# Later adaLN steps wait for the first FFN's norm and are spread over its down projections; one chunk's columns come within the output projection

## The chip, the core and the metric

One Trainium2 (trn2) chip, one core. The metric is the device time of one execution in microseconds (us); before the change it is 1256.7 us, the median of 3 runs (1254.57 to 1257.02).

## What is computed

A backbone of two layers over 512 latent tokens of width 1024, with 256 context tokens that feed only layer 0's keys and values. Layer 0 mixes with windowed grouped-query attention, layer 1 with a short gated convolution. Cut to what matters here:

```python
def layer(i, h, c, ...):
    sh1, sc1, g1, sh2, sc2, g2 = split(silu(c) @ ada_w[i] + ada_b[i], 6)     # adaLN: 6 chunks of 1024
    h = h + g1 * mixer_i(rms_norm(h, norm_mix[i]) * (1 + sc1) + sh1)
    a = rms_norm(h, norm_ffn[i]) * (1 + sc2) + sh2
    g, u = split(dwconv3(a @ w_up[i], ffn_conv[i]), 2)                      # w_up 1024 x 5632
    return h + g2 * ((silu(g) * u) @ w_down[i])                             # w_down 2816 x 1024
```

The change touches the adaLN vectors: per layer `silu(c)`, 1024 long, times a 1024 x 6144 matrix, in six chunks of 1024 outputs (0 and 1: shift and scale of the mixer's norm, 2: its gate, 3 and 4: shift and scale of the FFN's norm, 5: its gate).

## The kernel before, in words

All data are feature-major: the state `h` is eight tiles of 128 features x 512 tokens. A product in float32 is made of three TensorE (PE) matmuls on values split in a high and a low part (`mm3`, L196 to L198). So each weight that arrives (`wraw`, 128x1024) is split by ScalarE (ACT, `whi`, L164) and VectorE (DVE, `wlo`, L165) before PE can use it. With `n` pieces of 1024 inputs, one `proj` of one output tile of 128 x 512 is 8 x 3 matmuls.

**The adaLN vectors.** A chunk is made in eight steps, one per 128 inputs. A step loads two tiles `araw` of 128x512 (SP's queue, L244 in the FFN, L672 in attention, four buffers). GpSimd (POOL) multiplies each by a column of `silu(c)` (L258) and adds it to one of two accumulators `adaacc` (L260); a chunk's first step multiplies straight into the accumulator. When a chunk is done, PE transposes each half (four 128x128, L265, into the PSUM bank `qt`), and VectorE reduces it to columns and adds the bias (L270, L271, in `ada_columns`). Chunks 0 and 1 of layer 0 are made elsewhere. Chunks 2 to 4 of layer 0 (24 steps) are made within attention, chunk 5 of layer 0 and all six of layer 1 (56 steps, 112 tiles) within the first FFN.

**Attention** is written out by hand: the string `ORDER` names each step in the order in which the instructions are issued (`with tc.manual_schedule()`). In it `ad` loads an adaLN step, `ap` is the multiply and addition of one half, `AT` and `AR` are a half's transposes and columns; `T`, `C`/`c`, `V` are the probabilities' transposes, copies and value products; `Ri` or `ri` (ACT or GpSimd) spreads a pair's reciprocal denominators, which PE transposes (`RT`); `N`, `Nh`, `Nl` normalise a pair of heads and split the result, `Nl` on GpSimd (L666).

Everything after attention is ordered by the Tile scheduler, which takes instructions as they become ready and follows the program's order within that.

**Output projection** (`out_proj`). The first four output tiles come from weights that are in place (`lead`, 4 x 24 matmuls, kt by kt across the four), the other four in halves of 256 tokens (the tail), so that the norm of the first half (`norm_half`) begins while PE does the second. `sumsq_add` (L207) sums the squares of `h`, on GpSimd for output tiles 1 and 2 and on VectorE for the others. `rstd` makes the reciprocal root with matmuls over the features (L215) and transposes (L225), in layer 0's FFN norm by ACT's root and VectorE's reciprocal (L222), in later norms by VectorE and a power on GpSimd (L218, L219). `modulate` (L233 to L235) writes the normed, modulated activation in its two parts: VectorE, ACT, VectorE.

**First FFN** (`ffn`). 44 up projections in 22 pairs (gate and value), in thirds of 8, 8 and 6 pairs; after each third its part of the down projection, eight output tiles. The first two pairs run as four pieces in halves of the tokens, so that the norm's second half can be made beside the first. After each pair but the first, `tail0` calls three `ada_step`, as long as there are any, and at the pairs in `COLS_AT` it turns a finished chunk into columns. SP issues weights and adaLN tiles from one queue in the order that the scheduler has fixed, and a load of a tile waits there for its buffer.

Layer 1 has the same output projection, norm and first projection, with no adaLN steps beside them.

Of the kernel before, what the change touches and what calls it, by code (L numbers as in the profile page):

```python
# [41 lines left out]
for _k, _w in (("c", 16), ("gmix", 16), ("adab", 2 * 6 * KT), ("gffn", 16), ("fconv", 2 * 3 * 2 * NF), ("sconv", 3 * KT),  # L42
# [19 lines left out]
    wh5 qa0.2 kD0.0.0 Q1.1.0 kl0.0 qa0.3 qs0.3 wl5 kD0.0.1 kT1.1 kh1.1 ap2.0 hT0 kD1.1.0 qd0.3 wr9 Q1.0.1 wr10 hh0 kl1.1 hl0 kD1.1.1 Q1.0.2
    qp0.3 wl7 S0.0 wr11 Q1.0.3 M0.0.1 ap1.1 M0.0.0 E0.0.1 Q1.1.1 qr1.0 qs1.0 ap2.1 ad3 S0.1 E0.0.0 qd1.0 Q1.1.2 M0.1.0 qa1.0 ad4 Q1.1.3 M0.1.1
    E0.1.0 qp1.0 hT1 qr1.1 qs1.1 S0.3 E0.1.1 Q1.2.0 M0.3.0 ap3.0 hh1 Q1.2.1 M0.3.1 E0.3.0 hl1 E0.3.1 S0.2 qa1.1 qd1.1 Q1.2.2 M0.2.1 qp1.1 Q1.2.3
    M0.2.0 E0.2.1 Dd0 E0.2.0 ap4.0 S1.0 qr1.2 T0.0.1 De0 qs1.2 hT2 C0.0.1 M1.0.1 T0.0.2 qa1.2 hh2 V0.0.1 M1.0.0 C0.0.2 T0.0.3 ap3.1 E1.0.1 Rd0
# [865 lines left out]
```

## Time and profile before

| what | us |
|---|---|
| median of 3 runs | 1256.7 (1254.57 to 1257.02) |
| the profiled execution | 1254.22 |
| its span, first to last instruction | 1252.1 |
| mean granted TensorE clock of the span | 0.989 |
| busy: PE / DVE / ACT / POOL | 1208.0 / 762.5 / 480.5 / 399.1 |

The page splits the span by engines, then into 40 slices, then follows the chain of work that ended last. What is busy on the average says little here: TensorE is busy nearly throughout, and what it misses lies in a few stages. The stages in the text are read off the timeline of TensorE: attention ends at 245.43 us, the half-width tail of the output projection begins at 273.12, the first FFN projection ends at 342.63, and the half-width tail of the first FFN's last third begins at 685.13. Layer 1's counterparts are 859.11 (tail) and 907.53 (end of the first projection).

### The profile page before, as it was taken

How to read it: one execution, taken by the hardware profiler on the slowest of the kernel's cores; microseconds unless marked ns; L12 is line 12 of the kernel's file. 1: busy time of each engine (PE TensorE's matmuls, PEld its weight loads, DVE VectorE, ACT ScalarE, POOL GpSimd, SP SyncE). 2: the span in 40 equal slices, each digit the busy share in tenths (PEclk: the TensorE clock that was granted, in tenths of full speed). 3: DMA queues.
4: the chain of work that ended last, by engine and by line, in shares of the span. 5: the costliest groups of instructions: out<-in, count | busy, mean ns of one | idle time of the engine just before them, and what ended most of it. 6: DMA issues, size and time to landing. Idle time of an engine off the chain costs nothing.

```text
span 1252.1 us, 16546 instructions
## 1 busy us (share of the span) xinstructions
PE 1208.0 (96%) x6414; PEld 983.6 (79%) x6414; DVE 762.5 (61%) x1126; ACT 480.5 (38%) x785; POOL 399.1 (32%) x360
## 2 busy tenths in 40 slices
PE   8999999987699999979999999999999999999998
PEld 6677666677688788858888988889988888888888
DVE  3678877549987547763586754443686445553552
ACT  4435777614253223321333442232454224422430
POOL 0039757759905609996092000001000000000000
PEclk8999999999899999989999999999999999999999
DMA  9445322355444534556253233222243333332211
GB/s 365 153 132 167 119 81 87 123 183 166 162 160 128 192 92 155 191 193 209 86 168 104 83 118 101 93 93 69 68 138 97 101 92 94 101 102 85 80 38 68
DMA packets 58382, 157.61 MB, mean 126 GB/s; under 512 B 6592, under 2 KB 8640, under 8 KB 58304
## 3 DMA queue, kind: packets, MB, share of 16 engines
q1 hardware_dynamic: 58304, 156.56, 38.3%
q8 instruction: 50, 0.82, 0.3%
q14 instruction: 28, 0.23, 0.1%
HBM read 152.86 MB, written 2.10 MB: 124 GB/s over the span
## 4 chain that ended last, share of the span: by engine, by line
PE 78%; DVE 8%; POOL 8%; issue 2%; DMA 2%; ACT 1%; SPq 0%; POOLq 0%; DVEq 0%; ACTq 0%
PE ps_s L197 10%; PE ps_s L198 10%; PE ps_s L196 10%; PE ps_pt L198 5%; PE ps_pt L197 5%; PE ps_pt L196 5%; POOL adaacc L260 4%; PE ps_oa L655 3%; PE ps_pt L636 3%; PE ps_s L575 3%; PE ps_oa L197 3%; PE ps_qt L197 3%; PE ps_qt L198 3%; PE ps_qt L196 3%; PE ps_oa L196 3%; PE ps_oa L198 2%
## 5 line engine op out<-in xcount | busy, mean ns | idle before, releaser
L165 DVE TENSOR_TENSOR wlo<-wraw,whi 128x1024 fp32r<-128x1024 f32 (+2 forms) x194 | 230.3, 1195 | 168.2 <-ACT whi L164 163.2
L164 ACT CAST whi<-wraw 128x1024 fp32r<-128x1024 f32 (+2 forms) x194 | 183.3, 953 | 340.3 <-PE ps_s L197 141.6
L260 POOL TENSOR_TENSOR adaacc<-adaacc,araw 128x512 f32<-128x512 f32 x140 | 199.4, 1429 | 9.0
L197 PE MATMUL ps_s<-a,whi 128*128 128x512 f32 (+1 forms) x512 | 190.4, 372 | 7.4 <-DVE a L235 7.4
L196 PE MATMUL ps_s<-a,whi 128*128 128x512 f32 (+1 forms) x512 | 190.2, 371 | 0.0
L198 PE MATMUL ps_s<-a,wlo 128*128 128x512 f32 (+1 forms) x512 | 190.1, 371 | 0.0
L258 POOL TENSOR_SCALAR araw<-araw,cs 128x512 f32<-128x512 f32 x140 | 128.8, 922 | 11.8 <-DMA araw<-in_ada 11.7
L197 PEld LDWEIGHTS ps_s<-a,whi 128*128 128x128 f32 x512 | 97.1, 190 | 24.4 <-DVE a L235 8.4
L198 PEld LDWEIGHTS ps_s<-a,wlo 128*128 128x128 f32 x512 | 97.3, 190 | 16.2
L196 PEld LDWEIGHTS ps_s<-a,whi 128*128 128x128 f32 x512 | 97.1, 190 | 16.2
L196 PE MATMUL ps_s<-g,whi 128*128 128x512 f32 (+1 forms) x264 | 91.9, 348 | 0.0
L198 PE MATMUL ps_s<-g,wlo 128*128 128x512 f32 (+1 forms) x264 | 91.7, 347 | 0.0
L197 PE MATMUL ps_s<-g,whi 128*128 128x512 f32 (+1 forms) x264 | 91.6, 347 | 0.0
L196 PE MATMUL ps_pt<-a,whi 128*128 128x512 f32 (+1 forms) x240 | 88.9, 370 | 0.0
L197 PE MATMUL ps_pt<-a,whi 128*128 128x512 f32 (+1 forms) x240 | 88.8, 370 | 0.0
L198 PE MATMUL ps_pt<-a,wlo 128*128 128x512 f32 (+1 forms) x240 | 88.6, 369 | 0.0
L164 ACT CAST g<-f 128x512 fp32r<-128x512 f32 x52 | 32.3, 620 | 124.0 <-DVE f L812 123.4
L744 DVE SCALAR_TENSOR_TENSOR h<-ps_s,ada,h 128x512 f32<-128x512 f32 (+1 forms) x40 | 25.6, 644 | 79.9 <-PE ps_s L198 79.7
L584 DVE CUSTOM_DVE_ANT_0 e<-ps_s,mask,nsink 128x512 f32<-128x512 f32 (+1 forms) x64 | 53.8, 873 | 14.8 <-PE ps_s L575 13.6
L811 ACT ACTIVATE f<-f 128x512 f32<-128x512 f32 x44 | 27.8, 633 | 89.8 <-DVE f L735 89.7
L207 POOL TENSOR_TENSOR f<-f,t 128x512 f32<-128x512 f32 x6 | 9.4, 1571 | 161.9 <-ACT t L206 161.9
L258 POOL TENSOR_SCALAR adaacc<-araw,cs 128x512 f32<-128x512 f32 x20 | 15.4, 774 | 140.6 <-PE ps_qt L265 127.0
(282 smaller groups left out, 2618.9 us busy)
## 6 DMA issues: line engine op xcount, KB each, us to landing
wraw<-in_wup SPq DMA_DIRECT2D x88, 512.0 KB, 3.6
araw<-in_ada SPq DMA_DIRECT2D x160, 256.0 KB, 2.7
wraw<-in_wdown SPq DMA_DIRECT2D x32, 512.0 KB, 3.6
wraw<-in_wsc SPq DMA_DIRECT2D x24, 512.0 KB, 3.5
gw<-in_ada SPq DMA_DIRECT2D x16, 512.0 KB, 9.0
wraw<-in_wqkv SPq DMA_DIRECT2D x12, 512.0 KB, 5.6
wraw<-in_wdown SPq DMA_DIRECT2D x16, 384.0 KB, 3.1
wraw<-in_wo SPq DMA_DIRECT2D x8, 512.0 KB, 3.8
```

Of the source, the lines that this page charges most:

```text
L164: act.copy(out=hi, in_=raw)
L165: vec.tensor_tensor(out=lo, in0=raw, in1=hi.bitcast(F32), op=ALU.subtract)
L196: pe.matmul(out=ps, lhsT=wh, rhs=ah, start=start, stop=False)
L197: pe.matmul(out=ps, lhsT=wh, rhs=al, start=False, stop=False)
L198: pe.matmul(out=ps, lhsT=wl, rhs=ah, start=False, stop=stop)
L258: pool.tensor_scalar(out=w if kt else a, in0=w, scalar1=c_, scalar2=1.0, op0=ALU.mult, op1=ALU.mult)
L260: pool.tensor_tensor(out=a, in0=a, in1=w, op=ALU.add)
L575: pe.matmul(out=s[t][:, i, :w], lhsT=q2s[p][x][HALF[t], cl], rhs=KEYS[p // 4][(p // 2 + t) % 2][y][HALF[t], ks_], start=(n == 0), stop=(n ...
L584: vec.tensor_tensor_reduce(out=e[:, :n].rearrange("p (a b) -> p a b", a=np_), in0=s[:, :np_, :w], in1=mb.rearrange("p (a b) -> p a b", a=n ...
L636: pe.transpose(out=pt[:, q:q + P], in_=es[p, b, t][0][:, o:o + P], identity=ident)
L655: pe.matmul(out=r["po"][HALF[t], b0:b0 + n], lhsT=V[:, j, p // 2, :], rhs=pf[:, t * n:(t + 1) * n], start=first, stop=not r["left"])
L811: act.activation(out=cv[0], in_=cv[0], func=AF.Silu)
```

## The change

- `ORDER` is written anew. The 24 adaLN steps stand in another place, the transposes and columns of its third chunk (`AT2`, `AR2`: chunk 4, the scale of the FFN's norm) are no longer in it, and `Ri`/`ri` are dealt out otherwise (before GpSimd for pairs 1 to 6, now for 1, 4, 6 and 7). That chunk's accumulators are tiles of the `g` ring.
- Those transposes and columns come in `out_proj` behind the residuals of its first four output tiles (`cols`).
- The first multiply of the first FFN's steps that is ordered so by hand waits for the last VectorE instruction of that FFN's norm (`add_manual_dep`).
- In the first FFN two steps follow each pair, and one step follows each output tile of the down projections of the first two thirds (`after`). A finished chunk becomes columns two calls later.

Of `ORDER` one line and its counterpart; the rest of the diff is whole but for blank context:

```diff
-    c7.1.1 ap21.0 V7.1.4 ad22 V7.1.3 V7.1.1 N7 ad23 Nh7 Nl7 ap22.1 ap23.1 ap22.0 AT2.1 AR2.1 ap23.0 AT2.0 AR2.0
+    ap22.0 V6.1.1 M7.3.0 V6.1.5 V6.1.4 M7.3.1 E7.3.0 T7.0.0 ap23.0 T7.0.2 N6 E7.3.1 S7.2 c7.0.0 Nh6 c7.0.2 V7.0.0 Nl6 T7.0.1 M7.2.1 V7.0.2
...
+    Rc7 T7.1.5 c7.1.1 V7.1.2 C7.1.5 T7.1.4 V7.1.1 C7.1.4 V7.1.5 V7.1.4 N7 Nh7 Nl7
@@ modulate
-        vec.scalar_tensor_tensor(out=lo, in0=n, scalar=sh, in1=hi.bitcast(F32), op0=ALU.add, op1=ALU.subtract)
+        return vec.scalar_tensor_tensor(out=lo, in0=n, scalar=sh, in1=hi.bitcast(F32), op0=ALU.add, op1=ALU.subtract)
@@ ada_step
-            ada_mult_add(acc[half], raws[half], kt)
+            ins = ada_mult_add(acc[half], raws[half], kt)
+            after = adastate.pop("after", None)
+            if after is not None:
+                tc.add_manual_dep(ins.ins, after.ins.name, DEP, reason="the norm has VectorE's port for itself")
@@ ada_mult_add
-        pool.tensor_scalar(out=w if kt else a, in0=w, scalar1=c_, scalar2=1.0, op0=ALU.mult, op1=ALU.mult)
+        ins = pool.tensor_scalar(out=w if kt else a, in0=w, scalar1=c_, scalar2=1.0, op0=ALU.mult, op1=ALU.mult)
...
+        return ins
@@ ap_
-                accs[ch, hf] = ap.tile([P, 512], F32, tag="aacc", name=nm("adaacc"), bufs=2)
+                accs[ch, hf] = ap.tile([P, 512], F32, tag="aacc", name=nm("adaacc"), bufs=2) if ch < 2 else g(F32)
@@ norm_half
-                modulate(h[kt][:, hf], r, smod[:, n["slot"], kt:kt + 1], ...
+                n["end"] = modulate(h[kt][:, hf], r, smod[:, n["slot"], kt:kt + 1], ...
@@ out_proj
                     residual(m, ps[m], gate)
                     done(m, FULL)
+                cols()
             tail = 4 if nxt is not None or last else 0
             for m in range(len(lead), KT - tail):
                 ps = proj([wpiece(src(m), n)], ah, al)[0]
                 residual(m, ps, gate)
                 done(m, FULL)
+                if after is not None:
+                    after(1)
@@
-        scale_cols(smod[:, 2, :], ada[0][:, 4, :], pc("gffn", 0, 8))
+        def last_cols():
+            for hf in range(2):
+                ada_columns(0, 4, hf, ada_transpose(accs[2, hf]))
+            scale_cols(smod[:, 2, :], ada[0][:, 4, :], pc("gffn", 0, 8))
@@ ffn
-                    if tail is not None:
-                        tail(j)
+                    if tail is not None and j:
+                        tail(2)
...
-                out_proj(lambda m: wdown_d[layer, m, :, j0 * P:j1 * P], (j1 - j0) * P, hh, hl, gate, nx, fin)
+                out_proj(lambda m: wdown_d[layer, m, :, j0 * P:j1 * P], (j1 - j0) * P, hh, hl, gate, nx, fin, after=None if fin else tail)
@@
-        def tail0(j):
-            for _ in range(3 if j else 0):
+        def tail0(n):
+            late.append(len(adadone))
+            if late[-3] and adadone:
+                ada_cols()
+                late[-2:] = [v - 1 for v in late[-2:]]
+            if "first" not in adastate:
+                adastate["first"] = adastate["after"] = nf["end"]
+            for _ in range(n):
                 if fsteps:
                     ada_step(*fsteps.pop(0))
-            if j in COLS_AT:
-                ada_cols()
```

How the instructions move, at three places. Tiles carry a number of their own in each program; `L265` became `L269`, `L258` `L261`, `L260` `L263`, `L666` `L670`; `L244` and `L172` are the same.

TensorE, the lead of the output projection (L265/L269 are the transposes of chunk 4, `g_1768` and `g_2883` the attention's output). Before, in the lead's second kt, between its third and fourth output tile (the other set stands behind the first output tile of the third kt):

```order
L196 MATMUL ps_s_2963<-g_1768,whiA_1546 128x512
L197 MATMUL ps_s_2963<-g_1769,whiA_1546 128x512
L198 MATMUL ps_s_2963<-g_1768,wloA_1547 128x512
L265 MATMUL ps_qt_2885<-ident,adaacc_2505 128x128 x4
L196 MATMUL ps_s_2964<-g_1768,whiA_1586 128x512
```

With the change, at the lead's end and the beginning of the half-width tail:

```order
L196 MATMUL ps_s_2949<-g_2883,whiA_1604 128x512
L197 MATMUL ps_s_2949<-g_2884,whiA_1604 128x512
L198 MATMUL ps_s_2949<-g_2883,wloA_1605 128x512
L269 MATMUL ps_qt_3060<-ident,g_2287 128x128 x4
L196 MATMUL ps_oa_3075<-g_1540,whi_2913 128x256
```

The transposes moved from within the lead to behind it; the second set moved likewise, into the first piece of the tail.

GpSimd, from the last subtraction of attention (L666/L670) on; `adaacc_2505` and `adaacc_2544` belong to chunk 4, `adaacc_3643` and `adaacc_3644` to the first chunk of the first FFN. Before:

```order
L666 TENSOR_TENSOR g_2876<-t_2869,g_2875 128x512
L258 TENSOR_SCALAR araw_2863<-araw_2863,cs 128x512
L260 TENSOR_TENSOR adaacc_2505<-adaacc_2505,araw_2863 128x512
L258 TENSOR_SCALAR araw_2873<-araw_2873,cs 128x512
L260 TENSOR_TENSOR adaacc_2505<-adaacc_2505,araw_2873 128x512
L258 TENSOR_SCALAR araw_2861<-araw_2861,cs 128x512
L260 TENSOR_TENSOR adaacc_2544<-adaacc_2544,araw_2861 128x512
L258 TENSOR_SCALAR araw_2871<-araw_2871,cs 128x512
L260 TENSOR_TENSOR adaacc_2544<-adaacc_2544,araw_2871 128x512
L258 TENSOR_SCALAR adaacc_3643<-araw_3639,cs 128x512
L258 TENSOR_SCALAR adaacc_3644<-araw_3641,cs 128x512
```

With the change, from the last addition of chunk 4 (`g_2287` is one of its accumulators) on:

```order
L263 TENSOR_TENSOR g_2287<-g_2287,araw_2651 128x512
L670 TENSOR_TENSOR g_2787<-t_2766,g_2786 128x512
L612 COPY t_2840<-den_2604 128x512
L670 TENSOR_TENSOR g_2884<-t_2881,g_2883 128x512
L261 TENSOR_SCALAR araw_3647<-araw_3647,cs 128x512
L261 TENSOR_SCALAR araw_3649<-araw_3649,cs 128x512
L207 TENSOR_TENSOR f_2929<-f_2929,t_3049 128x512
L207 TENSOR_TENSOR f_2929<-f_2929,t_3053 128x512
L261 TENSOR_SCALAR adaacc_3643<-araw_3639,cs 128x512
L261 TENSOR_SCALAR adaacc_3644<-araw_3641,cs 128x512
L263 TENSOR_TENSOR adaacc_3643<-adaacc_3643,araw_3647 128x512
```

Chunk 4's last four tiles now stand ahead of the last subtraction, and of the FFN's steps only two multiplies stand ahead of the two sums of squares (L207). The multiply into `adaacc_3643` is the one that waits for the norm.

SP, the loads of the first FFN from its first adaLN tiles on (`wraw<-in_wup` are up-projection weights, one per projection). Before:

```order
L244 DMA araw_3655<-in_ada 128x512
L244 DMA araw_3657<-in_ada 128x512
L172 DMA wraw_3364<-in_wup 128x1024
L244 DMA araw_3743<-in_ada 128x512
L244 DMA araw_3745<-in_ada 128x512
L172 DMA wraw_3663<-in_wup 128x1024
L244 DMA araw_3751<-in_ada 128x512
L172 DMA wraw_3696<-in_wup 128x1024
```

With the change (`wraw_3941` is the last of eight weights that follow each other, `wraw_3364` the first; fifteen adaLN tiles follow, of which the last three stand here):

```order
L172 DMA wraw_3880<-in_wup 128x1024
L172 DMA wraw_3941<-in_wup 128x1024
L244 DMA araw_3735<-in_ada 128x512
```

```order
L244 DMA araw_4017<-in_ada 128x512
L244 DMA araw_4019<-in_ada 128x512
L244 DMA araw_4025<-in_ada 128x512
L172 DMA wraw_3972<-in_wup 128x1024
L244 DMA araw_4027<-in_ada 128x512
L244 DMA araw_4109<-in_ada 128x512
L244 DMA araw_4111<-in_ada 128x512
L172 DMA wraw_4033<-in_wup 128x1024
L172 DMA wraw_4064<-in_wup 128x1024
```

The first eleven weights now stand ahead of all but four adaLN tiles; the twelfth (`wraw_3972`) stands behind 19 of them and the thirteenth (`wraw_4033`) behind 22.

## Rows read from the trace of the kernel before

**Rows 1.** The page: busy time of two engines (share of the span, instructions), and the engines' shares of the chain of work that ended last.

```profile
PE 1208.0 (96%) x6414; PEld 983.6 (79%) x6414; DVE 762.5 (61%) x1126; ACT 480.5 (38%) x785; POOL 399.1 (32%) x360
...
PE 78%; DVE 8%; POOL 8%; issue 2%; DMA 2%; ACT 1%; SPq 0%; POOLq 0%; DVEq 0%; ACTq 0%
```

**Rows 2.** The view by stages: start and end, length, busy us of PE, its weight loads, DVE, ACT and POOL with their instructions, granted clock (1.00 is full), DMA share, GB/s.

```profile
84.00:245.40 161.40, 159.99 (x1142) 108.33 (x1140) 126.86 (x265) 105.55 (x230) 121.22 (x120) 1.00 0.35 110
245.40:273.10 27.70, 23.12 (x103) 18.21 (x102) 8.28 (x12) 5.58 (x7) 13.13 (x14) 1.00 0.60 200
273.10:342.80 69.70, 52.89 (x398) 51.05 (x397) 62.07 (x66) 23.11 (x46) 66.92 (x57) 0.93 0.50 166
342.80:682.00 339.20, 330.50 (x1459) 268.69 (x1459) 215.47 (x246) 116.77 (x156) 185.25 (x152) 0.99 0.47 154
859.10:907.50 48.40, 47.46 (x397) 47.04 (x396) 27.87 (x62) 18.03 (x38) 1.86 (x2) 1.00 0.18 56
```

**Rows 3.** What TensorE waited for between 240 and 600 us: total, number of waits, longest.

```profile
PE ps_oa L196 <- ACT g L164: 8.0, 2, 7.1
PE ps_s L197 <- DVE a L235: 7.4, 5, 2.5
PE ps_qt L265 <- POOL adaacc L260: 4.6, 2, 2.6
PE ps_pt L215 <- DVE f L207: 3.7, 1, 3.7
PE ps_qt L225 <- DVE rcol L222: 2.6, 1, 2.6
```

**Rows 4.** The same between 840 and 925 us (layer 1's output projection, norm and first projection).

```profile
PE ps_pt L225 <- POOL rcol L219: 0.5, 1, 0.5
PE ps_s L225 <- POOL rcol L219: 0.4, 1, 0.4
```

**Rows 5.** Timeline of TensorE: start, duration. The first 128x256 matmul of the output projection's tail and the first 128x512 matmul behind the first projection, in layer 0 and in layer 1; and the first matmuls of two projections that follow each other in the first FFN.

```profile
273.12 0.28 PE L196 MATMUL ps_oa<-g,whi 128*128 128x256 f32 x1
...
342.63 0.40 PE L196 MATMUL ps_s<-a,whi 128*128 128x512 f32 x1
...
472.81 0.39 PE L196 MATMUL ps_qt<-a,whi 128*128 128x512 f32 x1
...
478.25 0.39 PE L196 MATMUL ps_s<-a,whi 128*128 128x512 f32 x1
...
859.11 0.28 PE L196 MATMUL ps_s<-g,whi 128*128 128x256 f32 x1
...
907.53 0.40 PE L196 MATMUL ps_oa<-a,whi 128*128 128x512 f32 x1
```

**Rows 6.** VectorE by shape in layer 0's norm, 291 to 342 us: count, busy us, mean ns, idle time before.

```profile
L233 DVE SCALAR_TENSOR_TENSOR t<-h,smod,t 128x256 f32<-128x256 f32 x16 | 18.0, 1162 | 1.2 <-ACT t L227 1.2
L235 DVE SCALAR_TENSOR_TENSOR a<-t,ada,a 128x256 fp32r<-128x256 f32 x16 | 16.9, 1080 | 0.0
```

**Rows 7.** The same in layer 1's norm, 878 to 901.5 us.

```profile
L235 DVE SCALAR_TENSOR_TENSOR a<-t,ada,a 128x256 fp32r<-128x256 f32 x16 | 7.3, 481 | 0.5 <-ACT a L234 0.5
L233 DVE SCALAR_TENSOR_TENSOR t<-h,smod,t 128x256 f32<-128x256 f32 x16 | 6.9, 481 | 2.3 <-ACT t L227 2.3
```

**Rows 8.** GpSimd's additions L260 alone, in a stretch from a multiply's start to an addition's end: length of the stretch, busy us and number of the additions.

```profile
248.30:256.50 8.20, 5.09 (x4) 1.00 0.57 190
...
467.00:504.20 37.20, 23.27 (x14) 1.00 0.47 149
```

**Rows 9.** Timeline of GpSimd: the first multiply of a chunk in the first FFN, with its duration, and in brackets the idle time before it.

```profile
466.98 0.69 POOL L258 TENSOR_SCALAR adaacc<-araw,cs 128x512 f32<-128x512 f32 x1 [36.45 <-PE ps_qt L265]
```

**Rows 10.** Timeline of SP's queue: four adaLN tiles, with the time that issuing them took, and the weight behind them.

```profile
526.01 9.14 SPq L244 DMA_DIRECT2D araw<-in_ada  x4
535.24 0.38 SPq L172 DMA_DIRECT2D wraw<-in_wdown  x1
```

**Rows 11.** The chain of waits in the first FFN: start, duration.

```profile
535.24 4.70 DMA wraw<-in_wdown
...
540.01 1.06 ACT whi L164
...
541.10 1.46 DVE wlo L165
```

**Rows 12.** Timeline of TensorE behind its longest wait of the first FFN.

```profile
558.99 0.80 PE L196 MATMUL ps_oa<-g,whi 128*128 128x512 f32 x1 [7.14 <-ACT g L164]
559.58 0.63 PE L198 MATMUL ps_pt<-g,wlo 128*128 128x512 f32 x1
560.01 0.63 PE L196 MATMUL ps_pt<-g,whi 128*128 128x512 f32 x1
```

**Rows 13.** The view by stages again, one stretch of the first FFN.

```profile
467.00:504.00 37.00, 37.00 (x169) 30.25 (x168) 29.65 (x33) 13.96 (x20) 36.33 (x28) 1.00 0.47 149
```

**Rows 14.** VectorE by shape in the first FFN, 467 to 530 us, the instructions with two inputs in SBUF.

```profile
L165 DVE TENSOR_TENSOR wlo<-wraw,whi 128x1024 fp32r<-128x1024 f32 x11 | 17.5, 1595 | 9.6 <-ACT whi L164 9.6
L165 DVE TENSOR_TENSOR g<-f,g 128x512 fp32r<-128x512 f32 x5 | 5.6, 1122 | 3.4 <-ACT g L164 3.4
L812 DVE TENSOR_TENSOR f<-f,f 128x512 f32<-128x512 f32 x6 | 5.1, 857 | 0.1
```

**Rows 15.** Timeline of VectorE: the last modulate instructions of layer 1's norm.

```profile
900.04 0.89 DVE L235 SCALAR_TENSOR_TENSOR a<-t,ada,a 128x256 fp32r<-128x256 f32 x2 [0.18 <-ACT a L234]
```

More of the change, by code (lines that the diff above doesn't have):

```diff
@@ L9 @@
 F32R = mybir.dt.float32r
+DEP = mybir.DependencyInfo(mybir.DependencyClass.Sync, mybir.DependencyReason.DATA)
 AF = mybir.ActivationFunctionType
@@ L62 @@
[L62 to L65, printed above, removed]
@@ L751, in norm_half, with out_proj @@
             for kt in range(KT):
-                modulate(h[kt][:, hf], r, smod[:, n["slot"], kt:kt + 1], n["shift"][:, kt:kt + 1], n["ah"][kt][:, hf], n["al"][kt][:, hf])
-        def out_proj(src, n, ah, al, gate, nxt=None, last=False, lead=(), tail_w=None):
+                n["end"] = modulate(h[kt][:, hf], r, smod[:, n["slot"], kt:kt + 1], n["shift"][:, kt:kt + 1], n["ah"][kt][:, hf], n["al"][kt][:, hf])
+        def out_proj(src, n, ah, al, gate, nxt=None, last=False, lead=(), tail_w=None, after=None, cols=None):
             def done(m, cl):
@@ L788 @@
         lead_tail = [wpiece(None, 1024, raw) for raw in lead_raw]
-        scale_cols(smod[:, 2, :], ada[0][:, 4, :], pc("gffn", 0, 8))
         splits[:] = (3, 6)
+        def last_cols():
+            for hf in range(2):
+                ada_columns(0, 4, hf, ada_transpose(accs[2, hf]))
+            scale_cols(smod[:, 2, :], ada[0][:, 4, :], pc("gffn", 0, 8))
         nf = norm_begin(2, ada[0][:, 3, :])
-        out_proj(lambda m: wo_d[m], 1024, o_hi, o_lo, ada[0][:, 2, :], nf, False, lead, lead_tail)
+        out_proj(lambda m: wo_d[m], 1024, o_hi, o_lo, ada[0][:, 2, :], nf, False, lead, lead_tail, cols=last_cols)
         def ffn(layer, ah, al, tail, nxt, second):
@@ L816, in ffn, with after_ffn0 @@
                     hl.append(lo)
-                    if tail is not None:
-                        tail(j)
+                    if tail is not None and j:
+                        tail(2)
                 fin = third == 2
                 nx = nxt() if fin and nxt is not None else None
-                out_proj(lambda m: wdown_d[layer, m, :, j0 * P:j1 * P], (j1 - j0) * P, hh, hl, gate, nx, fin)
+                out_proj(lambda m: wdown_d[layer, m, :, j0 * P:j1 * P], (j1 - j0) * P, hh, hl, gate, nx, fin, after=None if fin else tail)
             return nx
+        late = [0, 0]
         fsteps = [(0, 5, kt) for kt in range(KT)] + [(1, ch, kt) for ch in (1, 0, 4, 3, 2, 5) for kt in range(KT)]
-        def tail0(j):
-            for _ in range(3 if j else 0):
+        def tail0(n):
[6 more added lines that the diff above has]
+            for _ in range(n):
                 if fsteps:
                     ada_step(*fsteps.pop(0))
-            if j in COLS_AT:
+        def after_ffn0():
+            assert not fsteps
+            while adadone:
                 ada_cols()
-        def after_ffn0():
-            assert not fsteps and not adadone
             scale_cols(smod[:, 3, :], ada[1][:, 1, :], pc("gmix", 8, 8))
```

60 lines of the change are left out of this document (31 added, 29 removed).

## The prediction

> **What bounds the kernel now.** I read the page first: TensorE is busy for 96% of the span and most of the last-ending chain is its own, but 8% of that chain is GpSimd (POOL) and 8% VectorE (DVE) [rows 1]. The question is in which stage they stand there. The view by stages answers it [rows 2]. In attention (84 to 245 us) PE misses 1.4 us of 161.4. In the lead of the output projection (245.4 to 273.1) it misses 4.6. From the half-width tail of that projection to the end of the first FFN projection (273.1 to 342.8, "the norm stage") it misses 16.8 of 69.7, with VectorE busy for 62.1, GpSimd for 66.9 and a granted clock of 0.93. In the rest of the first FFN (342.8 to 682) it misses 8.7.
>
> The waits give those losses a name [rows 3]: 4.6 us for two transposes of the adaLN accumulator (L265) that GpSimd has not finished; in the norm stage VectorE's modulated activations (L235, 7.4), GpSimd's or VectorE's sums of squares (L207, 3.7) and the reciprocal (L222, 2.6); and 8.0 us, of which 7.1 at once, for a split of a down-projection weight.
>
> Layer 1 runs the same norm stage at 859 to 907 us with GpSimd all but idle (1.86 us of 48.4 [rows 2]). There PE waits for two reciprocals, 0.5 and 0.4 us, and for nothing else [rows 4]. From the first 128x256 matmul of the tail to the first 128x512 matmul after the first projection it takes 907.53 - 859.11 = 48.42 us, in layer 0 342.63 - 273.12 = 69.51 [rows 5]. VectorE's two modulate instructions, of the same shape, take 1162 and 1080 ns in layer 0 [rows 6] and 481 and 481 ns in layer 1 [rows 7]. So the norm stage of layer 0 is bound by VectorE, and VectorE is slowed by what GpSimd does beside it.
>
> The Trainium skill, "SBUF — State Buffer", section "Who interferes with whom", says why: a VectorE instruction with two SBUF inputs and a GpSimd instruction that reads SBUF take turns at one port, each for its whole instruction. By that rule, the 481 against 1162 ns agree.
>
> **The change, part by part.** The sum is made against the profiled execution: 1254.22 us, span 1252.1, 2.5 us under the median of 1256.7.
>
> *Transposes of chunk 4 in the output projection.* Before, both stand within the lead, ahead of matmuls that could run, and wait 2.6 and 2.0 us. Now the first stands behind the lead's last matmul and the second within the first half-width piece; the lead alone is 96 matmuls, about 22 us at the 0.23 us from one start to the next that 24 matmuls in 478.25 - 472.81 = 5.44 us give [rows 5]. GpSimd's last addition of the chunk stands ahead of its last three attention instructions (two subtractions and a copy), where before four multiplies and additions stood behind the last subtraction. Both ready: **-4.6**. The columns are needed only by the modulation, some 20 us later; VectorE has 8.3 us of work in the 27.7 us of the lead [rows 2].
>
> *Order of attention.* The same 24 steps, four tiles' work earlier: about 4 x 2.05 = 8.2 us, by the four additions with their multiplies that end in 8.2 us at 248.3 to 256.5 [rows 8]. GpSimd is busy for 121 of 161 us there, so 40 us are free, and PE's matmuls are the same. I take **0**. Bounds: -2, since PE misses only 1.4 us there; +4, half of those four tiles' time, if one normalisation step waits for GpSimd behind them. ACT and GpSimd trade a few reciprocal copies (Ri, ri); ACT is not on PE's waits here: 0, within those bounds. More accumulator tiles (the third chunk's from the "g" ring) take away the wait of its first multiply for the transposes of the chunk before.
>
> *The manual wait.* The first dependent multiply of the FFN's steps waits for VectorE's last modulate instruction. Behind it on GpSimd's queue stand only other adaLN multiplies and additions: both L207 sums of squares are ahead of it, so nobody on the norm's path waits for it. GpSimd does 28 additions less beside the norm. The stage should fall to layer 1's 48.4 us, plus two things: its reciprocal goes through ACT and VectorE rather than VectorE and GpSimd (waits of 0.9 us in all in layer 1, up to 3.8 now [rows 3, 4]; 2.5 taken, so +1.6), and one set of transposes lies in it (+0.4). 50.4 against 69.5: **-19.1**. Bounds: -21.1 (as layer 1), and -9.6 if half of the slowness were from something else, such as weights arriving at the same time. I take the upper part since the shape, the count and the neighbours of the instructions are the same in the two layers. Two multiplies of 0.69 us slip ahead of the wait: under 1.4 us of overlap, left in the bounds.
>
> *The first FFN.* Before, three steps (six tiles) follow each pair of projections, 6 x 2.6 = 16 us of GpSimd for 2 x 5.44 = 10.9 us of PE, so GpSimd falls behind, and then idles up to 36 us until the next chunk's transposes give an accumulator back [rows 9]. SP issues weights and adaLN tiles in one queue: at 526.01 it spends 9.14 us on four tiles, each waiting for a buffer, and the down-projection weight behind them is issued at 535.24; arrival and its two halves take until 542.6 [rows 10, 11]. The same thing some 10 us later makes the 7.1 us wait, after which matmuls start 0.43 us apart instead of 0.23 [rows 12], about seven of them, 1.4 us. What can be won is 8.7 + 1.4 = 10.1.
>
> Now there are two steps to a pair and one to a down-projection piece. A chunk of 8 steps then stands beside 4 pairs or 8 pieces, 43.5 us of PE. GpSimd did such a chunk (14 additions, their multiplies, two first multiplies) in 37.2 us at 467 to 504 [rows 8], with VectorE at 29.7 of 37 us and PE never short [rows 13]. So it keeps up by 6 us a chunk. It starts about 6.6 us before the end of the first projection (layer 1's last modulate ends at 900.9, [rows 15], and its first projection at 907.5). The twelfth and thirteenth weights are the first that stand behind adaLN tiles: the thirteenth is issued when tile 18 is done, 14 x 2.66 + 4 us after GpSimd starts (two of the first four tiles need no addition, and two multiplies are done), so 34.6 us after the end of the first projection, and is usable after 4.7 + 1.1 + 1.5 more [rows 11]: 41.9, against 8 x 5.44 = 43.5. It fits, barely. I leave 0.9 us for a new wait there: **-9.2**.
>
> Sum: -4.6 + 0 - 19.1 - 9.2 = -32.9: 1221.3 against the profiled execution, **1224** against the median.
>
> **The rivals.**
> A: *The FFN stays paced by GpSimd's tiles.* For it: the margin of 1.6 us at the thirteenth weight, and one queue for weights and tiles. Against it: 6 us of slack per chunk. Then the 9.2 us are not won, or a little is lost: 1230 to 1238.
> B: *Attention's order costs time*, by a normalisation that waits on GpSimd or ACT, repeated over a few pairs: +4 to +10, so 1228 to 1234. Against it: PE's whole loss there is 1.4 us now.
> C: *More is won*: the norm stage equals layer 1's, and attention gains 2 us or some contention beside the lead: 1210 to 1216.
> D, the other side: *GpSimd and VectorE block each other through the whole first FFN.* GpSimd's seven chunks end with step 56, beside PE's pair 20; PE needs about 19 x 10.9 + 16 x 5.44 = 294 us until there, so with its start 6.6 us early and 7.3 us for the last weight, a chunk may take (294 + 6.6 - 7.3) / 7 = 41.9 us. Each us more costs 7. The kernel is slower than before from 41.9 + 32.9 / 7 = 46.6 us a chunk on. If every VectorE instruction with two SBUF inputs stopped GpSimd for its whole length, a chunk would be 14 x 2.05 + 1.4 = 30.1 us alone plus 4 x (2 x 1.60 + 1.12 + 0.86) = 20.7 [rows 14], 50.8 in all: 7 x 8.9 = +62, so 1286. Against it: under just that load the chunk took 37.2 us, so only about a third of this shows. The rule of the Trainium skill named above, taken so that GpSimd is always the loser, gives this case; "issue order decides who blocks" in the same section leaves room for the smaller number.
> E: *The wait does nothing*, since the two multiplies ahead of it, or VectorE's own work, hold the norm as before: 1254.2 - 13.8 + 2.5 = 1243.
>
> **How the numbers follow.** Forecast, 1216 to 1229: 0.66. A 0.16, B 0.05, C 0.07, D 0.04, E 0.02. The range 1214 to 1238 holds the forecast, A, B and the near half of C, about 0.88; I keep it there since each of the terms has its own bound (-21.1 to -9.6 for the norm alone). A measurement of this kernel tells 0.2%, 2.5 us, from no change. D alone is slower: 0.04. No case centres on no change; between E and D 0.02. Faster 0.94.
>
> **What would show it.** In the profile after: the norm stage at about 50 us with the modulate instructions near 480 ns and GpSimd idle beside them, PE's wait for L235 gone; no wait of the transposes behind the lead; GpSimd busy almost without a break for some 260 us from the norm's end, at 37 us a chunk; PE's waits for weight splits in the first FFN under 2 us. It would be wrong if modulate stayed above 800 ns with GpSimd idle, if GpSimd's tiles took over 3 us in the FFN and weights came late each pair, or if PE waited in attention for reciprocals.

## The result and the profile after

The changed kernel takes 1238.4 us (median of 4, 1237.1 to 1240.3) against 1256.9 for the kernel before: ratio 0.986, interval 0.984 to 0.988. The time fell, as forecast, and the interval lies clear of 1, but it fell by 18.5 us and not by 33: 1.5%, under the 2% from which a kernel counts as faster here. It lies 0.4 us above the range.

The split by stages shows where the forecast and the chip part. Each end is read off TensorE's timeline; those of before are in [rows 5] and, for the last, in the section on the profile before. The column "predicted" and the brackets give the change against before.

| stage | before | predicted | after |
|---|---|---|---|
| start of the output projection's tail | 273.12 | -4.6 | 265.38 (-7.7) |
| norm stage, tail to the end of the first projection | 69.51 | -19.1 | 47.69 (-21.8) |
| FFN, from there to the third down projection's tail | 342.50 | -9.2 | 355.55 (+13.1) |
| rest of the span | 566.97 | 0 | 566.98 |
| span | 1252.1 | -32.9 | 1235.6 (-16.5) |

Two terms came out better than predicted, by 5.8 us together. The third has the wrong sign, and it alone, 22 us, is more than the whole miss. That the time lies so near the range is owed to the first two.

TensorE's timeline in the kernel after: the tail, the end of the first projection, the longest wait of the FFN, the tail of the third down projection.

```profile
265.38 0.37 PE L196 MATMUL ps_oa<-g,whi 128*128 128x256 f32 x1
...
313.07 0.40 PE L196 MATMUL ps_s<-a,whi 128*128 128x512 f32 x1
...
395.31 1.09 PE L269 MATMUL ps_qt<-ident,adaacc 128*128 128x128 f32 x4 [15.39 <-DVE ada L274]
...
668.62 0.28 PE L196 MATMUL ps_oa<-g,whi 128*128 128x256 f32 x1
```

The view by stages of the kernel after: the lead, the norm stage, the FFN (columns as in [rows 2], which has the same stages of before).

```profile
243.00:265.40 22.40, 22.40 (x101) 18.09 (x99) 6.71 (x7) 5.98 (x8) 2.66 (x3) 1.00 0.59 210
265.40:316.00 50.60, 50.60 (x416) 50.05 (x414) 35.15 (x75) 24.42 (x50) 12.78 (x12) 1.00 0.36 110
313.07:668.62 355.55, 335.49 (x1474) 273.41 (x1473) 218.51 (x246) 117.78 (x157) 249.12 (x204) 0.97 0.51 166
```

In the lead and the norm stage PE misses nothing (before 4.6 and 16.8 us). In the FFN it misses 20.1 us (8.7 before), which is 11.4 of the 13.1 us that the stage grew; for the other 1.7 PE is busy, at a mean granted clock of 0.97 against 0.99 before [rows 2].

VectorE by shape in the norm, 283 to 311 us, answering to [rows 6]: the modulate instructions take 479 and 478 ns, where they took 1080 and 1162, and as long as layer 1's of [rows 7].

```profile
L235 DVE SCALAR_TENSOR_TENSOR a<-t,ada,a 128x256 fp32r<-128x256 f32 x16 | 7.3, 479 | 0.3 <-ACT a L234 0.3
L233 DVE SCALAR_TENSOR_TENSOR t<-h,smod,t 128x256 f32<-128x256 f32 x16 | 7.0, 478 | 0.9 <-ACT t L227 0.9
```

What TensorE waited for between 84 and 720 us, answering to [rows 3].

```profile
PE ps_qt L269 <- DVE ada L274: 18.7, 2, 15.4
PE ps_qt L554 <- POOL qr L545: 1.5, 1, 1.5
PE ps_pt L505 <- DVE e L497: 1.4, 1, 1.4
PE ps_oa L197 <- DVE g L165: 0.9, 1, 0.9
...
PE ps_oa L196 <- ACT g L164: 0.4, 1, 0.4
```

The waits for the modulated activations, the sums of squares and the split products (`g`, L164) are gone or under 1 us. Two new waits, L554 and L505, lie in attention, at 102.9 and 89.8 us. One more new name stands there: the transposes of a finished chunk, L269, 18.7 us in two waits, 15.39 of them at 380 to 395 us, where the first down projection begins. By the row PE waits for VectorE: the second half's transposes go into the bank `qt`, which holds the first half's until VectorE has reduced them (L274).

### The profile page after: what moved, and what is told of

Its sections match the earlier page's. It is cut to its first block, busy times and chain, and to the rows that moved or that the text cites. A ratio compares the mean times of both kernels' runs of the same rounds, so it can differ in the third digit from the quotient of the medians.

```text
span 1235.6 us, 16549 instructions
## 1 busy us (share of the span) xinstructions
PE 1198.8 (97%) x6414; PEld 980.6 (79%) x6414; DVE 735.1 (59%) x1128; ACT 478.4 (39%) x785; POOL 406.5 (33%) x358
## 4 chain that ended last, share of the span: by engine, by line
PE 77%; POOL 10%; DVE 6%; issue 3%; DMA 2%; ACT 2%; SPq 0%; POOLq 0%; ACTq 0%; DVEq 0%
PE ps_s L196 10%; PE ps_s L198 10%; PE ps_s L197 10%; PE ps_pt L198 5%; POOL adaacc L263 5%; PE ps_pt L197 5%; PE ps_pt L196 5%; PE ps_oa L659 3%; PE ps_pt L640 3%; POOL araw L261 3%; PE ps_oa L197 3%; PE ps_oa L198 3%; PE ps_qt L197 3%; PE ps_qt L198 3%; PE ps_qt L196 3%
## 5 line engine op out<-in xcount | busy, mean ns | idle before, releaser
L165 DVE TENSOR_TENSOR wlo<-wraw,whi 128x1024 fp32r<-128x1024 f32 (+2 forms) x194 | 225.9, 1172 | 190.3 <-ACT whi L164 185.2
L164 ACT CAST whi<-wraw 128x1024 fp32r<-128x1024 f32 (+2 forms) x194 | 183.4, 953 | 359.0 <-PE ps_s L197 148.3
L196 PE MATMUL ps_s<-a,whi 128*128 128x512 f32 (+1 forms) x512 | 189.2, 369 | 0.0
L263 POOL TENSOR_TENSOR adaacc<-adaacc,araw 128x512 f32<-128x512 f32 x126 | 177.8, 1417 | 7.3
L261 POOL TENSOR_SCALAR araw<-araw,cs 128x512 f32<-128x512 f32 x140 | 133.5, 957 | 26.5 <-DMA araw<-in_ada 26.5
L196 PEld LDWEIGHTS ps_s<-a,whi 128*128 128x128 f32 x512 | 96.5, 188 | 16.2
L196 PE MATMUL ps_s<-g,whi 128*128 128x512 f32 (+1 forms) x264 | 92.1, 349 | 0.0
L196 PE MATMUL ps_pt<-a,whi 128*128 128x512 f32 (+1 forms) x240 | 88.3, 368 | 0.0
L164 ACT CAST g<-f 128x512 fp32r<-128x512 f32 x52 | 32.3, 621 | 120.5 <-DVE f L824 119.9
L207 POOL TENSOR_TENSOR f<-f,t 128x512 f32<-128x512 f32 x6 | 10.5, 1751 | 201.3 <-ACT t L206 201.3
L748 DVE SCALAR_TENSOR_TENSOR h<-ps_s,ada,h 128x512 f32<-128x512 f32 (+1 forms) x40 | 25.6, 643 | 82.0 <-PE ps_s L198 81.9
L165 DVE TENSOR_TENSOR g<-f,g 128x512 fp32r<-128x512 f32 x52 | 45.3, 871 | 25.5 <-ACT g L164 25.5
L588 DVE CUSTOM_DVE_ANT_0 e<-ps_s,mask,nsink 128x640 f32<-128x640 f32 (+1 forms) x64 | 53.7, 874 | 11.2 <-PE ps_s L579 10.9
```

Source lines behind the costliest of these rows:

```text
L164: act.copy(out=hi, in_=raw)
L165: vec.tensor_tensor(out=lo, in0=raw, in1=hi.bitcast(F32), op=ALU.subtract)
L196: pe.matmul(out=ps, lhsT=wh, rhs=ah, start=start, stop=False)
L261: ins = pool.tensor_scalar(out=w if kt else a, in0=w, scalar1=c_, scalar2=1.0, op0=ALU.mult, op1=ALU.mult)
L588: vec.tensor_tensor_reduce(out=e[:, :n].rearrange("p (a b) -> p a b", a=np_), in0=s[:, :np_, :w], in1=mb.rearrange("p (a b) -> p a b", a=n ...
L748: vec.scalar_tensor_tensor(out=h[m][:, cl], in0=ps[:, cl], scalar=gate[:, m:m + 1], in1=h[m][:, cl], op0=ALU.mult, op1=ALU.add)
```

## Where the FFN's time goes

Why is VectorE so late with a reduction of 0.68 us? Follow it back from 394 us. SP's queue in the kernel after: fifteen adaLN tiles in a row, then the twelfth weight, three more tiles, then the thirteenth and fourteenth.

```profile
307.42 31.18 SPq L244 DMA_DIRECT2D araw<-in_ada  x15
338.71 0.37 SPq L172 DMA_DIRECT2D wraw<-in_wup  x1
...
342.09 0.84 SPq L172 DMA_DIRECT2D wraw<-in_wup  x2
```

GpSimd now starts on the FFN's steps at 306.7 us, and SP's fifteen loads go as fast as GpSimd frees four buffers: 31.18 us. So the twelfth weight is issued at 338.71. Its split on ACT and then on VectorE:

```profile
342.42 1.05 ACT L164 CAST whi<-wraw 128x1024 fp32r<-128x1024 f32 x1 [15.10 <-DMA wraw<-in_wup]
```

```profile
343.50 1.27 DVE L165 TENSOR_TENSOR wlo<-wraw,whi 128x1024 fp32r<-128x1024 f32 x1 [11.63 <-ACT whi L164]
344.69 0.68 DVE L824 TENSOR_TENSOR f<-f,f 128x512 f32<-128x512 f32 x1
348.86 1.60 DVE L165 TENSOR_TENSOR wlo<-wraw,whi 128x1024 fp32r<-128x1024 f32 x1 [3.49 <-ACT whi L164]
350.38 0.74 DVE L738 SCALAR_TENSOR_TENSOR f<-ps_s,par,f 128x511 f32<-128x511 f32 x1
...
394.48 0.68 DVE L274 TENSOR_REDUCE ada<-ps_qt 128x4 f32<-128x512 f32 x1
...
399.50 1.14 DVE L824 TENSOR_TENSOR f<-f,f 128x512 f32<-128x512 f32 x1
401.33 1.02 DVE L165 TENSOR_TENSOR g<-f,g 128x512 fp32r<-128x512 f32 x1 [0.69 <-ACT g L164]
```

ACT stands idle for 15.10 us and VectorE for 11.63 at the head of their queues. PE does not need that weight yet: it is at pairs 3 and 4 (counted from 0; the twelfth weight is pair 5's second), and runs without a gap until 379.9. But the split stands ahead of work that could run. VectorE's queue there, as the program orders it (`wlo_3975` is the twelfth weight, `wlo_4036` the thirteenth):

```
L165 TENSOR_TENSOR wlo_3975<-wraw_3972,whi_3974 128x1024
L824 TENSOR_TENSOR f_3721<-f_3721,f_3725 128x512
L165 TENSOR_TENSOR wlo_4036<-wraw_4033,whi_4035 128x1024
L738 SCALAR_TENSOR_TENSOR f_3817<-ps_s_3759,par,f_3817 128x511
```

Behind the splits wait the product of a pair that PE has finished (L824) and the convolution of the next (L738). From then on VectorE is behind PE, and it does not catch up: PE ends pairs 3 to 7 at 335.0, 345.9, 356.8, 367.7 and 378.5 us, and VectorE starts on their products (L824) at 357.1, 367.9, 378.2, 389.6 and 399.5, each time 21 to 22 us later. It shows nowhere on PE, since PE's next pieces need only weights, until the down projection: that needs the last pairs' split products (L165, the last at 401.33), and the transposes in front of it need the bank.

## Experiments

Theory 1 is the chain just told: late weights hold ACT and VectorE at the head of their queues, VectorE falls behind, PE pays at the turn to the down projection. Theory 2: the one bank `qt` at the turn is the cause, whatever the weights do. A third view, the rival D of the prediction, that GpSimd and VectorE block each other through the whole FFN, is read from the trace after below.

All are single executions with a profile unless an interval is given; the kernel before took 1256.2 to 1256.3 us beside them.

**Loads in turn.** In the changed kernel each load of an adaLN tile gets an edge (`ORD`, order on SP's queue alone) to the last weight load ahead of it in the program (`lastw`), the steps are dealt out otherwise, and a finished chunk's columns are made ahead of the first down projection (`drain`):

```diff
-            sp.dma_start(out=w, in_=ada_d[layer, ch, kt, :, half * 512:(half + 1) * 512])
+            ld = sp.dma_start(out=w, in_=ada_d[layer, ch, kt, :, half * 512:(half + 1) * 512])
+            tc.add_manual_dep(ld.ins, lastw[0].ins.name, ORD, reason="weights first")
...
-                        tail(2)
+                        tail(1 if j < 5 else 3 if j > 19 else 2)
+                if tail is not None and not third:
+                    drain()
```

> The changed kernel, with each adaLN load of the first FFN ordered on SP behind the last weight load that precedes it in the program, one step instead of two behind pairs 1 to 4 (three behind the last two pairs), and the first chunk's columns made at the latest ahead of the first down projection. So 8 adaLN tiles instead of 19 stand ahead of the twelfth weight. Theory 1 (the twelfth weight comes late behind fifteen tiles, ACT and VectorE wait for it at the head of their queues with the convolutions behind it, and PE pays for VectorE's lag at the first down projection): VectorE's 11.6 us of idle at 332 to 343 us and PE's 15.4 us at 380 to 395 us are gone; the FFN stage (first projection's end to the half-width tail of the third down projection) falls from 355.6 to 333 to 340 us, the kernel to 1218 to 1224 us. Theory 2 (PE waits because the second half's transposes need the one bank qt, whatever VectorE's weights do): the transposes still stand at the turn, a wait of over 10 us stays, the kernel takes 1233 to 1240 us.

Measured: 1226.4 us (ratio 0.976, 0.974 to 0.978); FFN stage 344.7 in the profiled execution, which took 1228.2. SP, VectorE and PE:

```profile
326.73 1.52 SPq L174 DMA_DIRECT2D wraw<-in_wup  x2
329.77 11.11 SPq L246 DMA_DIRECT2D araw<-in_ada  x4
340.98 0.85 SPq L174 DMA_DIRECT2D wraw<-in_wup  x2
```

```profile
345.96 2.34 DVE L166 TENSOR_TENSOR wlo<-wraw,whi 128x1024 fp32r<-128x1024 f32 x1 [6.58 <-ACT whi L165]
```

```profile
390.21 1.09 PE L272 MATMUL ps_qt<-ident,adaacc 128*128 128x128 f32 x4 [8.63 <-DVE ada L277]
```

The idle for the twelfth weight is gone. VectorE's longest idle is now 6.6 us instead of 11.6, and PE's wait 8.6 instead of 15.4. The rest stays because SP now stands for 11.11 us over the four tiles ahead of the fifteenth weight (340.98). The numbers lie between the two expectations and short of theory 1's; but the two waits fell together.

**The steps alone**, as above without the lines on `ld` that order the loads:

> As the kernel before it in this series, but without the order of the loads: only the steps are counted otherwise (one behind pairs 1 to 4, three behind the last two) and the first columns are made ahead of the first down projection. On SP fifteen tiles still stand between the eleventh and the twelfth weight. Theory 1: VectorE's idle of 11 to 12 us for the twelfth weight stays and PE waits 8 to 16 us at the turn; FFN stage 345 to 356 us. A rival (the number of steps in the first third is what counts): the wait is halved, FFN stage about 345 or less with VectorE's idle under 6 us.

1239.0 us, FFN stage 357.0, 1 us above theory 1's bound.

```profile
343.73 1.22 DVE L165 TENSOR_TENSOR wlo<-wraw,whi 128x1024 fp32r<-128x1024 f32 x1 [11.70 <-ACT whi L164]
```

```profile
394.78 1.09 PE L269 MATMUL ps_qt<-ident,adaacc 128*128 128x128 f32 x4 [14.13 <-DVE ada L274]
```

Dealing the steps out otherwise changes little: fifteen tiles stand in a row again, 31.19 us on SP. The order of the loads alone is worth 357.0 - 344.7 = 12.3 us.

**No columns.** The transposes and columns of the FFN's chunks left out:

```diff
-        layer, ch, acc = adadone.pop(0)
-        for half in range(2):
-            ada_columns(layer, ch, half, ada_transpose(acc[half]))
+        adadone.pop(0)
```

> The changed kernel without the transposes and columns of the seven chunks made in the first FFN (the columns are left at zero, the steps stay). Theory 1: PE still waits at the first down projection, now for the split products of pairs 6 and 7 that VectorE makes late: over 8 us at one or two places between 378 and 402 us, and VectorE's idle of 11 to 12 us at 332 us stays; FFN stage 350 us or more. Theory 2: PE's 18.7 us of waits for transposes are gone and nothing takes their place: FFN stage 333 to 338 us.

1286.2 us, FFN stage 403.4.

```profile
344.54 1.23 DVE L167 TENSOR_TENSOR wlo<-wraw,whi 128x1024 fp32r<-128x1024 f32 x1 [11.74 <-ACT whi L166]
```

```profile
392.07 0.80 PE L198 MATMUL ps_oa<-g,whi 128*128 128x512 f32 x1 [8.42 <-ACT g L166]
...
410.44 0.80 PE L198 MATMUL ps_oa<-g,whi 128*128 128x512 f32 x1 [15.28 <-ACT g L166]
```

With no transposes at all PE waits at the same turn for ACT's part of the split products, 8.42 and 15.28 us. So theory 2 falls: without the bank the wait stays, under another name. Only the first of the two compares with the changed kernel, since SP issues the last three down-projection weights later here (390.6 to 411.3 us, there all by 383.0). That the stage is 48 us longer than with the columns was not expected and was not followed to its end; SP's order changed with the columns (five waits of this kind, 44.1 us in all), so this run says what the wait is, not what it costs.

**No steps.** `fsteps = []`, so no adaLN work in the first FFN and zeros for its chunks:

> The changed kernel without any adaLN step in the first FFN (the seven chunks' columns are left at zero): the floor of the stage. If PE's own matmuls are all that is left, the FFN stage takes 330 to 333 us (before 342.5, changed 355.6) and the modulate instructions stay at 480 ns; the kernel takes 1211 to 1216 us. If VectorE or the weights bound the stage without GpSimd too, over 340 us.

1207.8 us. The FFN stage in the view by stages:

```profile
314.96:639.02 324.06, 324.06 (x1418) 265.85 (x1417) 180.19 (x216) 119.42 (x157) 3.36 (x2) 1.00 0.32 98
```

324.06 us with PE busy for all of it: a floor 6 us under the expected one, and the time 3 us under its range. What adaLN costs the FFN was 18.4 us before and is 31.5 after; the prediction had put what can be won at 10.1, which held only waits and the slow clock after them. VectorE starts on the products 3.6 us behind PE here.

**Fewer early.** As the first, with the steps dealt out so that the thirteenth and fourteenth weight stand behind 8 tiles instead of 12, and the fifteenth and sixteenth behind 12 instead of 16:

```diff
-                        tail(1 if j < 5 else 3 if j > 19 else 2)
+                        tail((0, 1, 1, 1, 1, 0, 2, 2)[j] if j < 8 else 3 if j > 17 else 2)
```

> The kernel with ordered loads again, with no step behind pair 5 and three behind each of the last four pairs, so that the twelfth to fourteenth weight stand behind 8 tiles and the fifteenth behind 12 (before: the twelfth behind 8, the thirteenth behind 12, where SP stood for 11.1 us over four tiles). Theory 1: VectorE no longer stands idle for the thirteenth weight (6 us of 10 at 340 to 350 us before), PE's 8.6 us wait for the transposes at the first down projection falls under 3, the FFN stage from 344.7 to 333 to 338 us, the kernel from 1226 to 1215 to 1220 us. Theory 2 (the one bank qt): over 6 us of that wait stay and the kernel stays at 1223 or more.

The expectation has a weight wrong: SP stood for 11.1 us ahead of the fifteenth, and the thirteenth had gone before that, at 326.73.

1225.0 us (ratio 0.976, 0.974 to 0.977), FFN stage 341.0 in the profiled execution, which took 1224.6. This is the lowest time of the kernels that compute everything, but by the medians only 1.4 us under loads in turn.

```profile
322.50 5.79 SPq L174 DMA_DIRECT2D wraw<-in_wup  x3
328.38 1.82 SPq L246 DMA_DIRECT2D araw<-in_ada  x4
330.30 1.57 SPq L174 DMA_DIRECT2D wraw<-in_wup  x2
```

```profile
339.69 1.70 DVE L166 TENSOR_TENSOR wlo<-wraw,whi 128x1024 fp32r<-128x1024 f32 x1 [3.24 <-ACT whi L165]
```

```profile
381.61 0.63 PE L272 MATMUL ps_qt<-ident,adaacc 128*128 128x128 f32 x4
...
387.86 0.50 PE L198 MATMUL ps_oa<-g,whi 128*128 128x512 f32 x1 [1.19 <-ACT g L165]
...
509.61 0.63 PE L272 MATMUL ps_qt<-ident,adaacc 128*128 128x128 f32 x4 [3.11 <-DVE ada L277]
```

VectorE's idle is 3.24 us and PE waits 1.19 at the turn; the second half's transposes stand there too (381.61) and wait for nothing. For the waits this is theory 1's prediction. The stage stays 3 us above its range, and the time 5 us: the second turn, at 510 us, has a wait of its own, 3.11 us. By the time alone, 1223 or more, theory 2 would hold as well; the wait of over 6 us that it asks for is not there. The accounts of the stage:

```profile
314.82:655.83 341.01, 334.57 (x1474) 271.56 (x1473) 220.18 (x246) 117.71 (x157) 250.30 (x204) 0.99 0.53 173
```

```profile
L272 PE MATMUL ps_qt<-ident,adaacc 128*128 128x128 f32 x56 | 8.6, 275 | 3.5 <-DVE ada L277 3.1 <-DVE f L742 0.3
```

341.0 is the floor of 324.1, plus 6.4 us idle, plus 8.6 of transposes, plus 1.9 that remains; the mean granted clock is 0.99 here and 1.00 there.

**No wait.** The changed kernel without the manual wait (`adastate["after"]` is not set):

> The changed kernel without the manual wait, all else as in it. Theory 1: the norm stage goes from 47.7 back to 62 to 70 us with the modulate instructions over 1000 ns, and the FFN stage falls from 355.6 to 335 to 346 us, since GpSimd has done some twenty tiles more by the norm's end and no fifteen tiles stand ahead of the twelfth weight; the kernel takes 1243 to 1252 us. A rival (the steps behind the down projections are what costs the FFN its time): the FFN stage stays at 350 us or more and the kernel takes over 1252 us.

1249.1 us: norm stage 73.3, longer than expected, FFN 339.9. VectorE in the norm:

```profile
L233 DVE SCALAR_TENSOR_TENSOR t<-h,smod,t 128x256 f32<-128x256 f32 x16 | 17.4, 1125 | 1.2 <-ACT t L227 1.2
L235 DVE SCALAR_TENSOR_TENSOR a<-t,ada,a 128x256 fp32r<-128x256 f32 x16 | 14.1, 898 | 0.2 <-ACT a L234 0.2
```

One of the two modulate instructions stays under the expected 1000 ns. The wait alone gives the norm its 25.6 us and costs the FFN 15.7. The steps behind the down projections gain a little without it: 339.9 against 343.8 with the old dealing out of the next experiment, which has the same attention. By the Trainium skill, "SBUF — State Buffer", section "Who interferes with whom", the VectorE instruction that finds GpSimd at the shared port stands still for GpSimd's whole instruction; 1125 and 898 ns with GpSimd's steps beside them and 478 without agree.

**Order only.** The kernel before with the new `ORDER` and the columns within the output projection:

> The kernel before with the new order of attention and the columns of chunk 4 within the output projection alone. The output projection's tail begins at 265 to 268 us (before 273.1, changed 265.4), the norm stage stays at 67 to 71 us and the FFN stage at 339 to 346 us, the kernel takes 1246 to 1251 us. By the prediction's own step it would have been 4.6 us, so 1252.

1252.7 us: tail at 266.8, norm stage 73.4, FFN 343.8. The norm stage is 2.4 us above its range and the time 1.7.

```profile
PE ps_oa L196 <- ACT g L164: 8.1, 2, 7.3
PE ps_s L197 <- DVE a L235: 7.0, 5, 2.0
PE ps_qt L196 <- DVE ada L274: 5.1, 1, 5.1
```

The tail comes 6.4 us earlier, and 3.9 go again in the norm stage: there a half-width piece of PE wants the bank `qt` while VectorE, slow beside GpSimd, has not reduced the transposes (the row `ps_qt L196 <- DVE ada`, 5.1 us). By the time, 3.6 us under the kernel before, the prediction's 4.6 was near for this part by itself.

**Wait only.** The kernel before with the manual wait:

> The kernel before with the manual wait alone. The tail begins at 273.1 us, the norm stage takes 47 to 49 us, and all that it gives is partly lost in the FFN: eighteen tiles in a row stand ahead of the twelfth weight, VectorE stands idle for it over 11 us and PE waits at the first down projection. Theory 1: FFN stage 352 to 366 us, the kernel 1243 to 1257 us. The rival (the steps behind the down projections cost the time): FFN stage 343 us as before, the kernel 1233 to 1237 us.

1264.3 us, slower than before: tail 270.8, norm stage 47.2, FFN 377.6.

```profile
312.24 34.52 SPq L245 DMA_DIRECT2D araw<-in_ada  x18
```

```profile
353.47 1.95 DVE L166 TENSOR_TENSOR wlo<-wraw,whi 128x1024 fp32r<-128x1024 f32 x1 [16.79 <-ACT whi L165]
```

```profile
398.52 1.08 PE L270 MATMUL ps_qt<-ident,adaacc 128*128 128x128 f32 x4 [33.03 <-DVE f L740]
```

Eighteen tiles in a row ahead of the twelfth weight, VectorE idle for 16.8 us, and PE waits 33.0 us; stage and time are beyond their ranges. The wait stands earlier than expected, in the projection of pair 6, where this kernel has the first chunk's transposes. Three more weights behind two to four tiles each hold VectorE for 6.2, 4.8 and 3.5 us there. Together, from the five kernels with steps and columns and the wait ("behind PE" is the time from PE's end of a pair to the start of its product on VectorE):

| kernel | tiles in a row ahead of the weight that VectorE waits for | VectorE's longest idle for a weight | VectorE behind PE, pairs 3 to 7 | PE's wait at the first turn | FFN stage |
|---|---|---|---|---|---|
| fewer early | 4 (SP stands 1.8) | 3.2 | 4.9 to 6.1 | 1.2 | 341.0 |
| loads in turn | 4 (SP stands 11.1) | 6.6 | 13.1 to 15.2 | 8.6 | 344.7 |
| changed kernel | 15 | 11.6 | 21.0 to 22.0 | 15.4 | 355.6 |
| steps alone | 15 | 11.7 | 20.3 to 22.0 | 14.1 | 357.0 |
| wait only | 18 | 16.8 | 23.0 to 38.3 (pairs 3 to 5) | 33.0 (in pair 6) | 377.6 |

The longer VectorE stood for the weight, the further it was behind PE and the longer PE waited; the changed kernel and steps alone are too near each other to be ranked.

## Why the prediction was wrong

- **The transposes, -4.6.** Right: their two waits are gone. The tail came 7.7 us earlier; the 3.1 beyond may be attention's, but two kernels with the same old order differ by 2.4 us at this point (273.1 and 270.8), so it is not told apart from the spread of the runs. The eight kernels with the new order have it at 265.4 to 267.3, on the mean 5.4 us before the two with the old.
- **Attention's order, 0.** Near it, by the same measure. But two waits of PE are new there, 1.5 and 1.4 us (L554 and L505). All eight kernels with the new order have them and neither with the old one. They cost up to 2.9 us; what was won against them was not followed.
- **The manual wait, -19.1.** The mechanism was right and the size a little low: -21.8, just past the bound of -21.1. The 1.6 us added for the reciprocal's other path and the 0.4 for transposes did not appear (of the 3.8 us quoted for that path [rows 3] shows 2.6): 47.7 is even under layer 1's 48.4.
- **The first FFN, -9.2.** This is the step that failed, at its last sentence but one: "It fits, barely." The stage took 13.1 us more instead of 9.2 less. The 0.9 us left for a new wait became two waits of 15.4 and 3.3 us. The sum compared the thirteenth weight's arrival with the moment when PE needs it. The weight came earlier than worked out (issued 29.0 us after the first projection's end, not 34.6) and PE never waited for it. What the sum left out is who else takes it: ACT and VectorE split weights in the order of their queues, ahead of convolutions of pairs that were done. The order that shows it, fifteen tiles between the eleventh and the twelfth weight on SP and the splits ahead of L824 and L738 on VectorE, was there to be read beforehand; the first half of it stands in the section on the change. With the loads in a better order (fewer early) 14.5 us of the 22.3 come back. The other 7.7 do not: PE still idles 6.4 us in that stage, where the prediction had left 0.9.

The sign was in the prediction's own rows. It took the 7.1 us wait of before for one on a weight's split; the row names ACT's `g`, the split of a product [rows 3, 12]. The trace of before shows the same chain there, in small. VectorE stands 5.41 us for the weight of [rows 11], with the convolutions of finished pairs behind it, and falls from 5.6 us behind PE to 11.1 and 10.8 for the last two pairs of the second third. So the last product's split comes late:

```profile
541.10 1.46 DVE L165 TENSOR_TENSOR wlo<-wraw,whi 128x1024 fp32r<-128x1024 f32 x1 [5.41 <-ACT whi L164]
...
558.32 0.62 ACT L164 CAST g<-f 128x512 fp32r<-128x512 f32 x1 [3.82 <-DVE f L812]
```

- **The rivals.** A, that the FFN stays paced by GpSimd's tiles, came nearest to what happened, with its place (the thirteenth weight) nearly right, but it was priced as a gain not won, or a little lost: the stage cost 13 us beyond the gain not won. D did not happen. GpSimd's timeline in the kernel after:

```profile
306.70 1.36 POOL L261 TENSOR_SCALAR adaacc<-araw,cs 128x512 f32<-128x512 f32 x2 [36.79 <-issue]
...
384.98 0.69 POOL L261 TENSOR_SCALAR adaacc<-araw,cs 128x512 f32<-128x512 f32 x1
...
396.50 1.54 POOL L261 TENSOR_SCALAR adaacc<-araw,cs 128x512 f32<-128x512 f32 x1 [9.49 <-PE ps_qt L269]
...
432.96 1.65 POOL L261 TENSOR_SCALAR adaacc<-araw,cs 128x512 f32<-128x512 f32 x1
```

From the third chunk's first multiply to the fourth's is 432.96 - 384.98 = 48.0 us, of which 9.49 is a wait for the transposes: 38.5 without it, near the 37.2 of [rows 8] and far from D's 50.8. Over all seven chunks (306.7 to 609.5 us) it is 43.3 us a chunk, above the 41.9 from which D decides, but 32.6 us in all are waits for transposes that PE makes late, and 38.6 a chunk is left. The kernel fewer early has the same work on GpSimd, 250.3 us busy beside the FFN against 249.1, and a stage 14.5 us shorter. E did not happen either: nothing of GpSimd's runs between 269.9 and 306.7. Two slips of the working move no term: GpSimd's longest idle time before is 43.2 us, not 36, and the chances named for the range add up to 0.90, not 0.88.
- **What was to be seen.** Modulate at 480 ns, no wait of the transposes behind the lead, splits of weights under 2 us: all came true, but the last by the letter only, since no wait for a weight's split stands in [rows 3] either and the stall that the splits caused went by another name. GpSimd was not busy without a break; it waits four times for transposes, 9.49 us of the 32.6 at 387 for those at the first turn, and its chunks end some 303 us after the norm, not 260.

## What to carry to other kernels

A weight that PE does not need yet can still stall the kernel: where its split stands at the head of ACT's and VectorE's queues, everything behind it waits, and the bill comes at the next place where PE depends on those engines. Here the lag was not made good on the way, since VectorE took as long for a pair as PE did (10.6 us on the mean, PE 10.9). So when loads are moved on a shared queue, compare their arrival with the first engine that takes them, in its own order, and not with the last. And a wait that makes one stage faster releases its work as a burst: the manual wait by itself won 22.3 us in the norm stage and lost 35.1 in the FFN. Look at what stands behind that burst in the queues of the next stage, and order it by hand where the scheduler puts the burst first.

## What was not expected of the hardware

GpSimd's steps cost PE much in the norm, where PE waits for VectorE, and little in the FFN: VectorE's modulate instructions took 2.3 times as long beside them, while in the FFN of the kernel fewer early, with GpSimd busy for 250 of 341 us, PE idled for 6.4. The order of loads on one queue decided 12.3 us of a kernel in whose FFN TensorE never waited for a weight.
